# Hybrid SSD and attention layer: order of the input norm's first tiles, of the forward pass's state, and of the DMA that adds the backward part

## The chip, the cores and the metric

One core of a Trainium2 chip runs the whole layer. The time is the device time of one execution in microseconds; several executions are measured and the median is given. The engines are TensorE (PE, matrix products, with PEld for its weight loads), VectorE (DVE), ScalarE (ACT), GpSimd (POOL) and SyncE (SP, which only issues DMAs). POOL issues DMAs as well; those that add into their destination are issued by POOL alone in this kernel.

## The reference

```python
h = rms_norm(x, norm_in_g)                       # x: 1024 tokens x 1024
proj = h @ w_in                                  # z, xbc, dt, q, k, v, ga
xbc = silu(conv5(xbc) + conv_b)                  # xs (1024), B and C (2 groups x 128)
dt = softplus(dt + dt_bias); A = -exp(a_log)
y = ssd(xs, dt_f, A_f, B, C)                     # chunks of 128, forward
  + rev(ssd(rev(xs), rev(dt_b), A_b, rev(B), rev(C)))   # backward
  + d_skip * xs
y_ssd = rms_norm(y * silu(z))                    # per group of 512
o = windowed_gqa(q, k, v, rel_bias, sink)        # 16 heads, 4 kv heads, window 128
y_attn = rms_norm(o * silu(ga))
out = rms_norm(x + concat(y_ssd, y_attn) @ w_out)
```

In `ssd`, chunk c gives `y(c) = M(c) xs(c) + exp(cs) C(c) S(c)`, with M the masked scores in the chunk, and the state goes on as `S(c+1) = decay * S(c) + B(c)^T (w * xs(c))`. All of it is float32.

## The kernel before, in words

The sequence of 1024 tokens is cut into 8 blocks (chunks) of 128. Every large product is made three times from float32r halves (hi·hi, hi·lo, lo·hi), so each operand is split: ACT copies to hi, DVE or POOL subtracts to lo (`load_split`, L129 to L138, for the weights: wraw, whi, wlo).

*Start.* SP loads x in eight tiles (`xts`: xt0, then pieces of the tile xk, xt5, CT, BT) and between them two weight pieces (after the second and third tile), L196 to L202. POOL issues six small DMAs ahead of its other work: four tables broadcast to 128 rows by `rows` (sink, dsk, dtb, Ab; L183 to L185), a mask msk (L192) and later rb (L188). For each tile of x the sum of squares ss is made (DVE for the first, L212, ACT for the others, L215), then the reciprocal root rs by `rsqrt` (DVE L117, POOL L118), and DVE scales the tile in place (L218). PE transposes it into PSUM banks (L220); two tiles share the banks; ACT makes hhi (L224) and DVE hlo (L225) from them, and four early projection halves follow on PE (L146).

*The two groups.* The SSD heads form two groups g of eight heads. For each group the conv makes xk, BT, CT, Bk, and d_skip's part goes to the scratch yb_d in DRAM (L532). A backward pass over the chunks (L574 to L584) adds its part to yb_d by a DMA that accumulates (L579). Then the forward pass (L620 to L657) does, for chunk c: `scores(c+1)` makes the next M (SP loads two tables cb by broadcast, L592; ACT and DVE work on them, L607 to L617); `y_off` multiplies C with the state S (PE L570) and DVE scales the result into the tile yb (L572); a DMA of POOL adds yb_d into yb (L630); the products y with M run on PE (L635) and DVE adds them to yb (L637); `advance` makes the next state: POOL weights xd (L542), ACT and DVE split it to xh and xl (L545, L546), PE makes three products (L552), POOL scales the old state (L557) and DVE adds (L558). At last POOL multiplies yb with the gate zt to yg (L643), which is stored to y_d (L644), ACT squares it (L646), POOL folds the squares to sqs (L647, L649), and PE sums four chunks' sqs at a time (`add_sums`, L519). In the first chunk, which has no state yet, SP loads yb from yb_d (L627).

`fill(n)` puts n half blocks of the remaining projections (24 products of PE each, "fills" below, L146) between these steps, so that PE has work while the chain of a chunk goes on. The attention and the output projection come after the second group.

The order on each engine isn't that of the code: a scheduler places the instructions by its own estimate of their times, and `tc.issue_after(i)` holds back what is written under it until instruction i is placed. Tiles come from pools with a number of buffers; a tile's next use waits until its last user is done. yb has three buffers, xh and xl one each, zt and yg one each.

Of the kernel before, what the change touches and what calls it, by code (L numbers as in the profile page):

```python
# [10 lines left out]
F32 = mybir.dt.float32  # L11
F32R = mybir.dt.float32r
AF = mybir.ActivationFunctionType
ALU = mybir.AluOpType
PSUM = bass.MemoryType.PSUM

P = 128
S = 1024
D = 1024
NSB = S // P  # L20
# [4 lines left out]
NH = 16  # L25
NKV = 4
EPS = 1e-6
NEG = -1e30
# [7 lines left out]
def kernel(  # L36
# [18 lines left out]
    nc = tc.nc  # L55
    V, A, G, T = nc.vector, nc.scalar, nc.gpsimd, nc.tensor
# [15 lines left out]
    yb_d = scratch("yb_d", [NG, NSB, P, 512], F32)  # L72
# [22 lines left out]
    nhalf = const.tile([P, 16], F32, name="nhalf")  # L95
# [19 lines left out]
    def rsqrt(dst, src, scale, eps):  # L115
        n = src.shape[1]
        V.tensor_scalar(out=dst, in0=src, scalar1=scale, scalar2=eps, op0=ALU.mult, op1=ALU.add)  # L117
        G.tensor_tensor(out=dst, in0=dst, in1=nhalf[:, 0:n], op=ALU.pow)  # L118


    pa = ctx.enter_context(ExitStack())
# [7 lines left out]
    def load_split(src, shape, wpool, tag="w", eng=None):  # L129
        raw = wpool.tile(shape, F32, tag=tag + "raw", name=tag + "raw", bufs=1 if tag != "w" else 3)  # L130
        nc.sync.dma_start(out=raw, in_=src)
        hi = wpool.tile(shape, F32R, tag=tag + "hi", name=tag + "hi")
        lo = wpool.tile(shape, F32R, tag=tag + "lo", name=tag + "lo")
        A.activation(out=hi, in_=raw, func=AF.Copy)  # L134
        nsplit[0] += 1
        eng = eng or (G if nsplit[0] % 3 == 0 else V)
        eng.tensor_tensor(out=lo, in0=raw, in1=hi.bitcast(F32), op=ALU.subtract)  # L137
        return hi, lo  # L138
# [27 lines left out]
    gp = pool(ssd, "gp", side="right")  # L166
# [8 lines left out]
    s1 = pool(s1c, "s1", side="right")  # L175
# [3 lines left out]
    def rows(t, src, n):  # L179
        G.dma_start(out=t, in_=bass.AP(tensor=src.tensor, offset=src.offset, ap=[[0, P], [1, n]]))  # L180
        return t

    both = rows(s1.tile([P, NH], F32, name="sink2"), sink, NH), rows(s1.tile([P, NH], F32, name="dsk2"), d_skip, NH)  # L183
    dtb = rows(s1.tile([P, 32], F32, name="dtb"), dt_bias, 32)
    Ab = rows(s1.tile([P, 32], F32, name="Ab"), a_log, 32)  # L185
    rb = s1.tile([64, NH], F32, name="rb")
    G.memset(rb, NEG)
    G.dma_start(out=rb[0:32], in_=rel_bias)  # L188

    dsk = gp.tile([P, NH // 2], F32, name="dsk")  # L190
    msk = gp.tile([P, 2, P], F32, name="msk")
    G.dma_start(out=msk, in_=c_tri)  # L192
    xts = [cp.tile([P, S + 4], F32, tag="pad", name="xt0")[:, 0:D]]
    xts += [tiles[3][:, 2 * i:2 * i + 2, :].rearrange("p b e -> p (b e)") for i in range(4)]
    xts += [cp.tile([P, S + 4], F32, tag="pad", name="xt5")[:, 0:D], tiles[1], tiles[0]]
    for sb, xt in enumerate(xts):  # L196
# [3 lines left out]
        if sb in (1, 2):  # L200
            blk = XBC0 + 6 + 2 * sb
            pre[blk] = load_split(w_blk[blk], [P, NKB, P], wp, eng=V)  # L202
    whi, wlo = load_split(w_vdt, [P, NKB, 288], s1, tag="wv", eng=G)
    for q in range(4):
        sh, o = divmod(q, 2)
        cols = slice(o * 256, o * 256 + 256)
        banks = [bank(t) for t in ("mm t s y", "t s t s", "t s t s", "t s y t")[q].split()]
        for j, xt in enumerate(xts[2 * q:2 * q + 2]):
            junk = cp.tile([P, D], F32, tag="acc", name="junk")
            ss = s1.tile([P, 1], F32, tag="ss", name="ss", bufs=8)  # L210
            if q == j == 0:
                V.tensor_tensor_reduce(out=junk, in0=xt, in1=xt, scale=1.0, scalar=0.0, op0=ALU.mult,  # L212
                                       op1=ALU.add, accum_out=ss)
            else:
                A.activation(out=junk, in_=xt, func=AF.Square, accum_out=ss)  # L215
            rs = s1.tile([P, 1], F32, tag="rs", name="rs", bufs=8)
            rsqrt(rs, ss, 1.0 / D, EPS)
            V.tensor_scalar(out=xt, in0=xt, scalar1=rs, scalar2=None, op0=ALU.mult)  # L218
            for kb in range(NKB):
                T.transpose(banks[kb // 2][:, (kb % 2) * 256 + j * P:(kb % 2) * 256 + (j + 1) * P],  # L220
                            xt[:, kb * P:(kb + 1) * P], ident)
        for kb in range(NKB):
            ps = banks[kb // 2][:, (kb % 2) * 256:(kb % 2) * 256 + 256]
            A.activation(out=hhi[sh][:, kb, cols], in_=ps, func=AF.Copy, scale=g_in[:, kb:kb + 1])  # L224
            V.scalar_tensor_tensor(out=hlo[sh][:, kb, cols], in0=ps, scalar=g_in[:, kb:kb + 1],  # L225
                                   in1=hhi[sh][:, kb, cols].bitcast(F32),
                                   op0=ALU.mult, op1=ALU.subtract)
        for blk, ws in pre.items():
            if o == 0:
                early.setdefault(blk, []).append(bank("mm"))  # L230
            for _ in proj_steps(early[blk][sh][:, cols], ws, sh, cols):
                pass
# [42 lines left out]
    with s1c:  # L275
# [4 lines left out]
        for sb in range(NSB):  # L280
            sh, j = divmod(sb, 4)
            ps = bank("mm")
            n = 0
            for kb in range(NKB):
                for l, r in ((hhi, whi), (hlo, whi), (hhi, wlo)):
# [9 lines left out]
                              in_=vt.bitcast(F32).rearrange("p k a d -> p k (a d)"))  # L295
# [20 lines left out]
        for d in range(2):  # L316
            V.scalar_tensor_tensor(out=dt[:, d], in0=t3v[:, :, d * NH:(d + 1) * NH], scalar=2.0,
                                   in1=t2v[:, :, d * NH:(d + 1) * NH], op0=ALU.mult, op1=ALU.add)
            V.scalar_tensor_tensor(
                out=av[:, d], in0=dt[:, d], scalar=-1.0,  # L320
                in1=Ab[:, d * NH:(d + 1) * NH].unsqueeze(1).broadcast_to([P, NSB, NH]),
                op0=ALU.mult, op1=ALU.mult)
# [200 lines left out]
    for g in range(NG):  # L523
# [16 lines left out]
        def weighted(c, d):  # L540
            xd = sp.tile([P, 512], F32, tag="xd", name="xd")
            G.tensor_tensor(out=v3(xd), in0=v3(xk[:, c, :]), in1=bc(hb(wst, d, c, g), 64), op=ALU.mult)  # L542
            xh = sp.tile([P, 512], F32R, tag="xh", name="xh", bufs=1)
            xl = sp.tile([P, 512], F32R, tag="xl", name="xl", bufs=1)
            A.activation(out=xh, in_=xd, func=AF.Copy)  # L545
            V.tensor_tensor(out=xl, in0=xd, in1=xh.bitcast(F32), op=ALU.subtract)  # L546
            return xh, xl, xh

        def advance(Sold, c, d):
            ps = bank("s")  # L550
            for i, (b, x) in enumerate(zip((Bk[0], Bk[0], Bk[1]), weighted(c, d))):
                T.matmul(ps, lhsT=b[:, c, :], rhs=x, start=i == 0, stop=i == 2)  # L552
            Sn = sp.tile([P, 512], F32, tag="S", name=f"S{d}")
            if Sold is None:
                A.activation(out=Sn, in_=ps, func=AF.Copy)
            else:
                G.tensor_tensor(out=v3(Sn), in0=v3(Sold), in1=bc(hb(dec, d, c, g), 64), op=ALU.mult)  # L557
                V.tensor_tensor(out=Sn, in0=Sn, in1=ps, op=ALU.add)  # L558
            return Sn
# [25 lines left out]
        Sf = None  # L585
# [35 lines left out]
        for c in range(NSB):  # L621
            M = Mn
            if c < NSB - 1:
                Mn = scores(c + 1)
            yb = sp.tile([P, 512], F32, tag="yo", name="yb", bufs=3)
            if Sf is None:
                nc.sync.dma_start(out=yb, in_=yb_d[g, c])  # L627
            else:
                y_off(Sf, c, 0, yb)
                G.dma_start(out=yb, in_=yb_d[g, c], accum_op=ALU.add)  # L630
            fill(FORWARD[c][0])
            py = bank("y")
            for h in range(HPG):
                a = h % 2 * 64
                T.matmul(py[a:a + 64, h // 2 * P:(h // 2 + 1) * P], lhsT=xk[:, c, h * 64:(h + 1) * 64],  # L635
                         rhs=M[:, h, :], start=True, stop=True)
            V.tensor_tensor(out=yb, in0=py, in1=yb, op=ALU.add)  # L637
            if c < NSB - 1:
                Sf = advance(Sf, c, 0)
            zt = sp.tile([P, 4, P], F32, tag="zt", name="zt", bufs=1)  # L640
            nc.sync.dma_start(out=zt, in_=z_d[g * 4:(g + 1) * 4, :, c * P:(c + 1) * P].rearrange("b p s -> p b s"))
            yg = sp.tile([P, 512], F32, tag="yg", name="yg", bufs=1)
            G.tensor_tensor(out=yg, in0=yb, in1=zt.rearrange("p b s -> p (b s)"), op=ALU.mult)  # L643
            nc.sync.dma_start(out=y_d[g, c], in_=yg)  # L644
            y2 = sp.tile([P, 512], F32, tag="y2", name="y2", bufs=1)
            A.activation(out=y2, in_=yg, func=AF.Square)  # L646
            G.tensor_tensor(out=y2[:, 0:256], in0=y2[:, 0:256], in1=y2[:, 256:512], op=ALU.add)  # L647
            sqs = sp.tile([P, P], F32, tag="sqs", name="sqs", bufs=6)
            G.tensor_tensor(out=sqs, in0=y2[:, 0:P], in1=y2[:, P:256], op=ALU.add)  # L649
            sums.append((g, c, sqs))  # L650
            if c == 5:
                add_sums()
            if g == NG - 1 and c == 4:
                load_kv(0, 0)
                load_q(0, 0)
                load_q(0, 1)
            fill(FORWARD[c][1])  # L657
# [403 lines left out]
```

## Time and profile before

| | |
|---|---|
| median of 3 runs | 907.78 us (905.4 to 909.92) |
| profiled execution | 908.26 us |
| its span | 906.5 us |
| mean granted clock of PE | 0.98 |
| PE busy | 94% of the span, 4622 instructions |
| DVE, ACT, POOL busy | 69%, 52%, 33% |

The span runs from the first to the last instruction on the chip; the profiled execution's own time is some 2 us longer, for what lies around it. A granted clock of 1.00 is PE's upper level, 2.4 GHz, and 0.5 its lower, 1.2 GHz; a mean between them over a stretch says how much of it ran at the lower level. Times within the span are counted from its start.

### The profile page before, as it was taken

Reading aid. Unit: us, or ns where it says so; the run is one execution under the profiler, and the core shown is the slowest. Engines: PE = TensorE matmul, PEld = TensorE weight load, DVE = VectorE, ACT = ScalarE, POOL = GpSimd, SP = SyncE. Lnnn points to the kernel's source line nnn. Section 1 sums busy time; section 2 is a strip of 40 time slices with the busy share of each in tenths; the row PEclk is TensorE's granted clock in tenths of the full one; section 3 lists DMA queues with packets and bytes.
Section 4 is the critical chain, followed back from the end, with each engine's and each line's share of the span. In section 5 each row is a group of like instructions: output and inputs, shape, how many; then the busy total and the mean of one; then the engine's idle time right before and its main releaser. Section 6 shows DMA issues by size and latency. Waiting matters only on the chain.

```text
span 906.5 us, 13315 instructions
## 1 busy us (share of the span) xinstructions
PE 853.0 (94%) x4622; PEld 720.2 (79%) x4622; DVE 623.7 (69%) x1035; ACT 469.3 (52%) x1078; POOL 296.6 (33%) x271
## 2 busy tenths in 40 slices
PE   4999999998998999999969999999999899898997
PEld 3998788886777888888857888877888688787886
DVE  4575665696898476447869936687888877875533
ACT  5632573453666345423645536766566566753222
POOL 4301012534764201234268450130441340432501
PEclk9999999999899999999988999999999999998999
DMA  8122563576888413678859859789656637422421
GB/s 301 67 83 58 180 213 121 150 211 182 228 240 267 127 46 93 160 195 195 223 147 278 223 184 283 211 231 307 181 151 190 187 108 189 159 63 96 148 81 49
DMA packets 127407, 154.24 MB, mean 170 GB/s; under 512 B 42331, under 2 KB 79899, under 8 KB 127212
## 3 DMA queue, kind: packets, MB, share of 16 engines
q1 hardware_dynamic: 121420, 141.35, 50.9%
q0 software_dynamic: 5776, 11.79, 7.4%
q8 instruction: 36, 0.59, 0.3%
q14 instruction: 31, 0.25, 0.1%
q10 hardware_dynamic: 144, 0.26, 0.1%
HBM read 111.58 MB, written 43.88 MB: 171 GB/s over the span
## 4 chain that ended last, share of the span: by engine, by line
PE 64%; DVE 13%; DMA 12%; issue 4%; ACT 2%; POOL 2%; SPq 1%; POOLq 0%; DVEq 0%; ACTq 0%
PE mm L146 30%; PE mm L695 17%; PE y L913 4%; PE s L877 3%; DMA cb<-cs_d 3%; PE mm L286 3%; PE t L891 2%; DMA yb<-yb_d 2%; DMA oraw<-in_w_out_dram 2%; DVE hlo L434 2%; DMA zt<-z_d 2%; DMA yb_d<-yo 1%; DMA xk<-in_x_dram 1%; PE s L570 1%; DVE M L616 1%
## 5 line engine op out<-in xcount | busy, mean ns | idle before, releaser
L146 PE MATMUL mm<-hhi,whi 128*128 128x512 f32 (+1 forms) x640 | 248.1, 390 | 1.5 <-ACT hhi L224 1.5
L146 PE MATMUL mm<-hlo,whi 128*128 128x512 f32 (+1 forms) x640 | 247.4, 388 | 0.2 <-DVE hlo L225 0.2
L146 PE MATMUL mm<-hhi,wlo 128*128 128x512 f32 (+1 forms) x640 | 247.1, 387 | 0.0
L146 PEld LDWEIGHTS mm<-hlo,whi 128*128 128x128 f32 x640 | 122.3, 191 | 23.0 <-issue 1.7
L146 PEld LDWEIGHTS mm<-hhi,whi 128*128 128x128 f32 x640 | 121.9, 192 | 23.4 <-ACT hhi L224 2.2
L146 PEld LDWEIGHTS mm<-hhi,wlo 128*128 128x128 f32 x640 | 122.4, 191 | 22.1 <-issue 0.7
L695 PE MATMUL mm<-hlo,yh 128*128 128x512 f32 (+1 forms) x264 | 105.8, 401 | 0.0
L695 PE MATMUL mm<-hhi,yl 128*128 128x512 f32 (+1 forms) x264 | 105.8, 401 | 0.0
L695 PE MATMUL mm<-hhi,yh 128*128 128x512 f32 (+1 forms) x264 | 105.8, 401 | 0.0
L883 ACT ACTIVATE lg<-lg,nm 128x320 f32<-128x320 f32 (+2 forms) x128 | 68.7, 537 | 41.5 <-DVE nm L880 39.4
L250 DVE SCALAR_TENSOR_TENSOR acc<-pad,prm_sb,acc 128x1024 f32<-128x1024 f32 x48 | 62.1, 1300 | 24.7 <-ACT acc L247 23.3
L880 DVE CUSTOM_DVE_ANT_0 lg<-s,bias,nsnk 128x320 f32<-128x320 f32 (+2 forms) x128 | 64.4, 519 | 21.3 <-PE s L877 20.5
L134 ACT ACTIVATE whi<-wraw 128x1024 fp32r<-128x1024 f32 x38 | 40.0, 1054 | 40.7 <-PE mm L146 37.7
L137 POOL TENSOR_TENSOR wlo<-wraw,whi 128x1024 fp32r<-128x1024 f32 x12 | 30.2, 2516 | 89.9 <-ACT whi L134 89.9
L695 PEld LDWEIGHTS mm<-hhi,yl 128*128 128x128 f32 x264 | 50.9, 193 | 5.9
L695 PEld LDWEIGHTS mm<-hlo,yh 128*128 128x128 f32 x264 | 51.1, 193 | 5.8
L607 ACT ACTIVATE cb<-cb,ncs 128x128 f32<-128x128 f32 x128 | 39.4, 390 | 31.0 <-DMA cb<-cs_d 28.9
L695 PEld LDWEIGHTS mm<-hhi,yh 128*128 128x128 f32 x264 | 50.8, 193 | 5.6
L137 DVE TENSOR_TENSOR wlo<-wraw,whi 128x1024 fp32r<-128x1024 f32 x26 | 33.8, 1298 | 23.4 <-ACT whi L134 20.8
L897 DVE TENSOR_TENSOR pl<-t,ph 128x512 fp32r<-128x512 f32 (+1 forms) x64 | 40.8, 652 | 9.1 <-ACT ph L896 8.4
L877 PE MATMUL s<-khh,qt 128*128 128x320 f32 (+1 forms) x128 | 39.7, 316 | 6.9 <-DVE nm L880 6.9
L941 POOL DMA_DIRECT2D rd_d<-rdt x8 | 4.4, 555 | 116.2 <-ACT rdt L940 116.2
(232 smaller groups left out, 1766.9 us busy)
## 6 DMA issues: line engine op xcount, KB each, us to landing
wraw<-in_w_blk_dram SPq DMA_DIRECT2D x38, 512.0 KB, 4.0
cb<-cs_d SPq DMA_DIRECT2D x32, 512.0 KB, 5.8
qt<-q_d SPq DMA_DIRECT2D x32, 256.0 KB, 4.0
oraw<-in_w_out_dram SPq DMA_DIRECT2D x32, 256.0 KB, 3.8
et<-es_d SPq DMA_DIRECT2D x56, 128.0 KB, 4.9
yb_d<-pad SPq DMA_DIRECT2D x8, 512.0 KB, 3.8
z_d<-gz SPq DMA_DIRECT2D x16, 256.0 KB, 3.8
zt<-z_d SPq DMA_DIRECT2D x16, 256.0 KB, 3.6
```

Of the source, the lines that this page charges most:

```text
L134: A.activation(out=hi, in_=raw, func=AF.Copy)
L137: eng.tensor_tensor(out=lo, in0=raw, in1=hi.bitcast(F32), op=ALU.subtract)
L146: yield T.matmul(ps, lhsT=l[:, kb, :], rhs=r[sh][:, kb, cols], start=(n == 0), stop=(n == 3 * NKB - 1))
L250: V.scalar_tensor_tensor(out=acc, in0=pad[:, k:k + S], scalar=cw[:, blk * 6 + k:blk * 6 + k + 1], in1=acc, op0=ALU.mult, op1=ALU.add)
L286: T.matmul(ps[:, 0:288], lhsT=l[sh][:, kb, j * P:(j + 1) * P], rhs=r[:, kb, :], start=(n == 0), stop=(n == 3 * NKB - 1))
L607: A.activation(out=E[:, h, :], in_=E[:, h, :], func=AF.Identity, bias=ncs[:, 0, c, hh:hh + 1])
L695: yield T.matmul(ps[:, cols], lhsT=l[:, j * P:(j + 1) * P], rhs=r[:, dh * 512 + cols.start:dh * 512 + cols.stop], start=first and n == 0, ...
L877: pe(lambda: T.matmul(ps[:, 0:c1 - c0], lhsT=self.qt[:, sub, 2 * hp:2 * hp + 2, :], rhs=kt[:, k0:k0 + c1 - c0], start=(i == 0), stop=(i == ...
L880: V.tensor_tensor_reduce(out=l, in0=ps[:, d0 - c0:d1 - c0], in1=bias[:, hp, d0 - f0:d1 - f0], scale=-1.0, scalar=nsnk[:, sk], op0=ALU.add, ...
L883: A.activation(out=l, in_=l, func=AF.Exp, scale=-1.0, bias=nm, accum_out=sm)
L897: V.tensor_tensor(out=pl[0:w, 0:n], in0=ps[0:w, 0:n], in1=ph[0:w, 0:n].bitcast(F32), op=ALU.subtract)
L913: pe(lambda: T.matmul(self.po[:, sub * 256:(sub + 1) * 256], lhsT=v, rhs=r[0:v.shape[0], c:c + 256], start=i == 1 and n == 0 and j == 0, s ...
```

## The change

Three things are moved.

1. The small tables' DMAs are issued by a function, `small_tables`, under `issue_after` of the first tile's root; and every further tile's root and scale are held until the tile before is scaled.
2. In the forward pass `advance` is written right behind `y_off`, ahead of the fills and of the products y. xh and xl get two buffers.
3. The DMA that adds yb_d into yb comes after the products' add, right ahead of the load of zt and of yg. The first chunk has no SP load any more: DVE copies its products to yb, and the DMA adds yb_d to them like in the other chunks.

```diff
     def rsqrt(dst, src, scale, eps):
...
-        G.tensor_tensor(out=dst, in0=dst, in1=nhalf[:, 0:n], op=ALU.pow)
+        return G.tensor_tensor(out=dst, in0=dst, in1=nhalf[:, 0:n], op=ALU.pow)
...
+    def small_tables():
+        both = rows(s1.tile([P, NH], F32, name="sink2"), sink, NH), rows(s1.tile([P, NH], F32, name="dsk2"), d_skip, NH)
+        dtb = rows(s1.tile([P, 32], F32, name="dtb"), dt_bias, 32)
+        Ab = rows(s1.tile([P, 32], F32, name="Ab"), a_log, 32)
+        rb = s1.tile([64, NH], F32, name="rb")
+        G.memset(rb, NEG)
+        G.dma_start(out=rb[0:32], in_=rel_bias)
+
+        dsk = gp.tile([P, NH // 2], F32, name="dsk")
+        msk = gp.tile([P, 2, P], F32, name="msk")
+        G.dma_start(out=msk, in_=c_tri)
+        return both, dtb, Ab, rb, dsk, msk
...
             rs = s1.tile([P, 1], F32, tag="rs", name="rs", bufs=8)
-            rsqrt(rs, ss, 1.0 / D, EPS)
-            V.tensor_scalar(out=xt, in0=xt, scalar1=rs, scalar2=None, op0=ALU.mult)
+            with ExitStack() as st:
+                if scaled is not None:
+                    st.enter_context(tc.issue_after(scaled.ins))
+                root = rsqrt(rs, ss, 1.0 / D, EPS)
+                scaled = V.tensor_scalar(out=xt, in0=xt, scalar1=rs, scalar2=None, op0=ALU.mult)
+            if q == j == 0:
+                with tc.issue_after(root.ins):
+                    both, dtb, Ab, rb, dsk, msk = small_tables()
...
-            xh = sp.tile([P, 512], F32R, tag="xh", name="xh", bufs=1)
-            xl = sp.tile([P, 512], F32R, tag="xl", name="xl", bufs=1)
+            xh = sp.tile([P, 512], F32R, tag="xh", name="xh")
+            xl = sp.tile([P, 512], F32R, tag="xl", name="xl")
...
             yb = sp.tile([P, 512], F32, tag="yo", name="yb", bufs=3)
-            if Sf is None:
-                nc.sync.dma_start(out=yb, in_=yb_d[g, c])
-            else:
+            first = Sf is None
+            if not first:
                 y_off(Sf, c, 0, yb)
-                G.dma_start(out=yb, in_=yb_d[g, c], accum_op=ALU.add)
+            if c < NSB - 1:
+                Sf = advance(Sf, c, 0)
             fill(FORWARD[c][0])
...
-            V.tensor_tensor(out=yb, in0=py, in1=yb, op=ALU.add)
-            if c < NSB - 1:
-                Sf = advance(Sf, c, 0)
+            if first:
+                V.tensor_copy(yb, py)
+            else:
+                V.tensor_tensor(out=yb, in0=py, in1=yb, op=ALU.add)
+            G.dma_start(out=yb, in_=yb_d[g, c], accum_op=ALU.add)
             zt = sp.tile([P, 4, P], F32, tag="zt", name="zt", bufs=1)
```

The order on DVE at the start, before. xt0 is the first tile of x, xk the next pieces, rs their roots, wlo the two early weight pieces.

```order
L117 TENSOR_SCALAR rs_171<-ss_169 128x1
L117 TENSOR_SCALAR rs_186<-ss_184 128x1
L218 TENSOR_SCALAR xt0_134<-xt0_134,rs_171 128x1024
L137 TENSOR_TENSOR wlo_143<-wraw_140,whi_142 128x1024
L218 TENSOR_SCALAR xk_116<-xk_116,rs_186 128x1024
L117 TENSOR_SCALAR rs_271<-ss_269 128x1
L218 TENSOR_SCALAR xk_116<-xk_116,rs_271 128x1024
L137 TENSOR_TENSOR wlo_150<-wraw_147,whi_149 128x1024
L225 SCALAR_TENSOR_TENSOR hlo0_101<-mm_164,prm_sb_76,hhi0_99 128x256
```

The same place after the change (the lines of the new file are some ten higher).

```order
L117 TENSOR_SCALAR rs_157<-ss_155 128x1
L225 TENSOR_SCALAR xt0_120<-xt0_120,rs_157 128x1024
L117 TENSOR_SCALAR rs_186<-ss_184 128x1
L137 TENSOR_TENSOR wlo_129<-wraw_126,whi_128 128x1024
L137 TENSOR_TENSOR wlo_136<-wraw_133,whi_135 128x1024
L225 TENSOR_SCALAR xk_116<-xk_116,rs_186 128x1024
L117 TENSOR_SCALAR rs_271<-ss_269 128x1
L225 TENSOR_SCALAR xk_116<-xk_116,rs_271 128x1024
L117 TENSOR_SCALAR rs_286<-ss_284 128x1
L235 SCALAR_TENSOR_TENSOR hlo0_101<-mm_150,prm_sb_76,hhi0_99 128x256
```

The first tile's scale now stands ahead of the second's root, and both wlo ahead of the second tile's scale.

The order on ACT at the start, before: the squares (junk, ss), the hi halves of the weight pieces and the first pieces of hhi.

```order
L215 ACTIVATE junk_183,ss_184<-xk_116 128x1024
L134 ACTIVATE whi_142<-wraw_140 128x1024
L215 ACTIVATE junk_268,ss_269<-xk_116 128x1024
L134 ACTIVATE whi_149<-wraw_147 128x1024
L224 ACTIVATE hhi0_99<-mm_164,prm_sb_76 128x256
L224 ACTIVATE hhi0_99<-t_165,prm_sb_76 128x256
L215 ACTIVATE junk_283,ss_284<-xk_116 128x1024
L224 ACTIVATE hhi0_99<-s_166,prm_sb_76 128x256
```

And after.

```order
L219 ACTIVATE junk_183,ss_184<-xk_116 128x1024
L134 ACTIVATE whi_128<-wraw_126 128x1024
L219 ACTIVATE junk_268,ss_269<-xk_116 128x1024
L134 ACTIVATE whi_135<-wraw_133 128x1024
L219 ACTIVATE junk_283,ss_284<-xk_116 128x1024
L219 ACTIVATE junk_366,ss_367<-xk_116 128x1024
L234 ACTIVATE hhi0_99<-mm_150,prm_sb_76 128x256
L234 ACTIVATE hhi0_99<-t_151,prm_sb_76 128x256
L219 ACTIVATE junk_381,ss_382<-xt5_121 128x1024
```

Two more squares now stand ahead of the first piece of hhi; the two later ones in the old order stood between its pieces.

The order on POOL at the end of the second forward pass (g = 1, chunks 5 to 7), before. yb_4447, yb_4562 and yb_4672 are the tiles yb of chunks 5, 6 and 7, S0 the state.

```order
L630 DMA yb_4562<-yb_d_66 128x512
L643 TENSOR_TENSOR yg_4483<-yb_4447,zt_4481 128x512
L647 TENSOR_TENSOR y2_4486<-y2_4486 128x256
L649 TENSOR_TENSOR sqs_4489<-y2_4486 128x128
L643 TENSOR_TENSOR yg_4634<-yb_4562,zt_4632 128x512
L647 TENSOR_TENSOR y2_4637<-y2_4637 128x256
L649 TENSOR_TENSOR sqs_4640<-y2_4637 128x128
L137 TENSOR_TENSOR wlo_4783<-wraw_4780,whi_4782 128x1024
L630 DMA yb_4672<-yb_d_66 128x512
L643 TENSOR_TENSOR yg_4731<-yb_4672,zt_4729 128x512
L647 TENSOR_TENSOR y2_4734<-y2_4734 128x256
L649 TENSOR_TENSOR sqs_4737<-y2_4734 128x128
```

And after, from chunk 5's yg on.

```order
L655 TENSOR_TENSOR yg_4483<-yb_4447,zt_4481 128x512
L659 TENSOR_TENSOR y2_4486<-y2_4486 128x256
L661 TENSOR_TENSOR sqs_4489<-y2_4486 128x128
L651 DMA yb_4562<-yb_d_66 128x512
L655 TENSOR_TENSOR yg_4634<-yb_4562,zt_4632 128x512
L659 TENSOR_TENSOR y2_4637<-y2_4637 128x256
L661 TENSOR_TENSOR sqs_4640<-y2_4637 128x128
L137 TENSOR_TENSOR wlo_4783<-wraw_4780,whi_4782 128x1024
L651 DMA yb_4672<-yb_d_66 128x512
L655 TENSOR_TENSOR yg_4731<-yb_4672,zt_4729 128x512
L659 TENSOR_TENSOR y2_4734<-y2_4734 128x256
L661 TENSOR_TENSOR sqs_4737<-y2_4734 128x128
```

Each accumulating DMA stood a chunk ahead of the yg that reads its tile; now yg stands right behind it. On PE, the last product of `add_sums` (L519 on the last chunk's sqs) stood 33 fills behind the last y products of this pass; now 51 fills and four short products of the attention (L877) lie between them.

## Rows read from the trace of the kernel before

**Rows 1.** The page, part 1: busy time of each engine.

```profile
PE 853.0 (94%) x4622; PEld 720.2 (79%) x4622; DVE 623.7 (69%) x1035; ACT 469.3 (52%) x1078; POOL 296.6 (33%) x271
```

**Rows 2.** Timeline of DVE at the start: start, duration, operation, idle before.

```profile
12.95 0.74 DVE L218 TENSOR_SCALAR xk<-xk,rs 128x1024 f32<-128x1024 f32 x1
...
17.02 1.22 DVE L137 TENSOR_TENSOR wlo<-wraw,whi 128x1024 fp32r<-128x1024 f32 x1
```

**Rows 3.** Timeline of ACT at the start.

```profile
14.27 1.06 ACT L215 ACTIVATE junk<-xk 128x1024 f32<-128x1024 f32 x1 [2.57 <-DMA xk<-in_x_dram]
...
16.31 0.46 ACT L224 ACTIVATE hhi<-mm,prm_sb 128x256 fp32r<-128x256 f32 x1
```

**Rows 4.** Timeline of POOL at the start.

```profile
5.64 0.56 POOL L118 TENSOR_TENSOR rs<-rs,nhalf 128x1 f32<-128x1 f32 x1 [1.01 <-DVE rs L117]
```

**Rows 5.** Windows at the start: busy time by engine, granted clock, DMA share, GB/s.

```profile
4.00:9.00 5.00, 0.00 (x0) 0.00 (x0) 1.42 (x4) 0.00 (x0) 1.88 (x7) 1.00 0.81 232
...
14.00:22.00 8.00, 6.24 (x25) 5.14 (x25) 5.80 (x14) 7.73 (x16) 1.73 (x5) 1.00 1.03 415
```

**Rows 6.** Windows of the two forward passes, and of projections between them.

```profile
212.00:290.00 78.00, 69.12 (x394) 55.30 (x393) 65.50 (x71) 43.53 (x107) 49.51 (x40) 0.96 0.80 233
...
432.00:537.00 105.00, 97.21 (x525) 78.82 (x523) 77.75 (x92) 57.08 (x138) 58.80 (x49) 0.95 0.77 210
...
300.00:325.00 25.00, 25.00 (x116) 20.78 (x115) 14.01 (x13) 9.53 (x12) 2.54 (x3) 1.00 0.32 90
```

**Rows 7.** Waits of PE, 187 to 300 us: line, releaser, total, times, longest.

```profile
PE y L635 <- DVE yb L637: 2.4, 1, 2.4
PE s L570 <- DVE S L558: 2.3, 2, 1.9
PE y L635 <- DVE M L617: 2.0, 1, 2.0
```

**Rows 8.** Waits of PE, 432 to 540 us.

```profile
PE y L635 <- DVE yb L637: 3.0, 2, 1.8
...
PE s L570 <- DVE S L558: 1.9, 1, 1.9
```

**Rows 9.** Line L630, the accumulating DMA: time from issue to landing.

```profile
DMA to landing us min/median/max: 4.1/5.8/7.2
```

**Rows 10.** Waits of DVE, 187 to 300 us.

```profile
DVE cb L608 <- DMA cb<-cs_d: 6.0, 4, 2.6
DVE wlo L137 <- POOL y L647: 2.5, 1, 2.5
```

**Rows 11.** Groups of POOL, 432 to 537 us: count, busy us, mean ns, idle before.

```profile
L643 POOL TENSOR_TENSOR yg<-yb,zt 128x512 f32<-128x512 f32 x8 | 13.9, 1734 | 15.6 <-DVE yb L637 13.5 <-DMA zt<-z_d 2.0
L557 POOL TENSOR_TENSOR S<-S,dec 128x512 f32<-128x512 f32 x7 | 11.4, 1628 | 3.3 <-ACT S L555 2.6 <-DVE S L558 0.6
L647 POOL TENSOR_TENSOR y<-y 128x256 f32<-128x256 f32 x8 | 8.3, 1043 | 4.5 <-ACT y L646 4.5
L649 POOL TENSOR_TENSOR sqs<-y 128x128 f32<-128x128 f32 x8 | 7.7, 962 | 0.4
L542 POOL TENSOR_TENSOR xd<-xk,wst 128x512 f32<-128x512 f32 x6 | 6.6, 1092 | 5.0 <-DVE xl L546 5.0
...
L137 POOL TENSOR_TENSOR wlo<-wraw,whi 128x1024 fp32r<-128x1024 f32 x2 | 5.2, 2586 | 0.0
```

**Rows 12.** Timeline of POOL at the end of the second forward pass.

```profile
533.72 1.27 POOL L643 TENSOR_TENSOR yg<-yb,zt 128x512 f32<-128x512 f32 x1 [5.23 <-DVE yb L637]
535.72 0.74 POOL L647 TENSOR_TENSOR y<-y 128x256 f32<-128x256 f32 x1 [0.74 <-ACT y L646]
536.54 0.46 POOL L649 TENSOR_TENSOR sqs<-y 128x128 f32<-128x128 f32 x1
```

**Rows 13.** Timeline of PE: first y products and last sum, second forward pass.

```profile
459.37 1.09 PE L635 MATMUL y<-M,xk 128*64 128x128 f32 x16 [1.81 <-DVE yb L637]
...
537.06 0.38 PE L519 MATMUL t<-ones,sqs 128*128 128x1 f32 x2
```

More of the change, by code (lines that the diff above doesn't have):

```diff
@@ L181, in rows @@
         return t
[L183 to L192, printed above, removed]
+    def small_tables():
[9 more added lines that the diff above has]
+        return both, dtb, Ab, rb, dsk, msk
     xts = [cp.tile([P, S + 4], F32, tag="pad", name="xt0")[:, 0:D]]
@@ L203 @@
     whi, wlo = load_split(w_vdt, [P, NKB, 288], s1, tag="wv", eng=G)
+    scaled = None
     for q in range(4):
```

## The prediction

> **What bounds the kernel now.** The page's first part comes first: TensorE (PE) is busy 853.0 us of the span's 906.5, DVE 623.7, POOL 296.6 [rows 1]. So what a change can win from PE is its 53 us of idle time and the time at its lower clock, and one asks where those lie in the stretches that the change touches: the start and the two forward passes.
>
> The start is read from the timelines. DVE ends x1's scale at 13.7 and spends 1.22 us on the second weight piece's lo after it [rows 2]. ACT has waited 2.57 us for x2 when it squares it at 14.27, and makes its first piece of hhi at 16.31 [rows 3]. POOL takes the first root at 5.64, behind the issues of the small tables [rows 4]. While these move, transfers run at 232 GB/s (4 to 9 us), against 415 GB/s in 14 to 22 us [rows 5].
>
> The forward passes are read from the windows and then from the waits. In 212 to 290 (first group, "g0" below) PE is busy 69.12 of 78 us at a granted clock of 0.96, DVE 65.50, POOL 49.51; in 432 to 537 (second group, "g1") PE 97.21 of 105 at 0.95 [rows 6]. PE waits there for yb, for the state S and once for M: in g0 2.4, 2.3 and 2.0 us, in g1 3.0 for yb and 1.9 for S [rows 7, 8]. Behind the first two stands one thing: DVE's add at L637 waits for the accumulating DMA, which lands 4.1 to 7.2 us after its issue, 5.8 in the middle [rows 9], and the state's add L558 and the next M are queued behind it on DVE. In 300 to 325, where PE never waits, its granted clock is 1.00 [rows 6].
>
> **The change part by part.** The profiled execution took 908.26 us, 0.5 over the median of the three runs; the sum is made against 908.3. About 0.5% (903.2 to 912.3) is what a measurement of this kernel can tell from no change.
>
> *Start.* Every row of x and every weight is still loaded, scaled and split; only the order moves. x0's scale leaves the wait for x1's root, which alone gains nothing: the first hhi reads a bank that holds x0 and x1. What counts is x1. It gains if the tables, issued behind the first root from 6.2 us on (5.64 + 0.56) [rows 4], no longer slow its load; the root loses nothing, since only the tables stand behind it on POOL. x1 loses in two places of the new order: the second lo of 1.22 us, and so the second weight piece's arrival, is now ahead of its scale on DVE, and two more squares of 1.06 us are ahead of the first hhi on ACT [rows 2, 3]. Best case: 5 us at 232 instead of 415 GB/s are 2.2 us of transfers, and as much again behind them: some −4. Worst case: all arrives as before, so the second hi ends at 16.4 (14.27 + two operations of 1.06), its lo at 17.6, x1's scale of 0.74 at 18.4 instead of 13.7, and the first hhi begins some 0.5 later, 18.9 instead of 16.3: +2.6. I take −1, near the middle, since the squares made early aren't made later between pieces of hhi.
>
> The rows show that loads are slow while the tables move, not where the tables would cost less. The Trainium skill ("DMA: Bandwidth & Descriptors", section "Issuing engines are not separate DMA queues") says that DMAs of all issuing engines run on the same 16 DMA engines and interleave. By that the tables cost their time wherever they stand, the second weight piece would be hit in x1's place, and the start would be the worst case; rows 5 agree in that the sum of both kinds of transfer falls to 232 GB/s.
>
> *State early.* On PE the three products of advance now come right behind y_off; on DVE the state's add no longer stands behind the add of yb. The waits addressed in g0 are 2.4 + 2.3 + 2.0 = 6.7 us, and the lower clock costs (1 − 0.96) × 78 = 3.1: together 9.8. In g1: 3.0 + 1.9 + (1 − 0.95) × 105 = 10.1. Not all of it can come. PE at full clock needs 69.12 − 3.1 = 66.0 us of the 78 in g0, DVE 65.50, so two nearly equal engines take turns; and DVE waits 6.0 us for the cb tables and 2.5 for a weight split [rows 10], so that it alone would need 74.0, 4.0 less than the 78. Between nothing and 9.8 I take half, near that: −4.9 in g0, and −5.0 in g1.
>
> *Second buffers for xh and xl.* ACT may write the next xh before PE has read the last. PE's waits for xl are not counted in the sum, neither gone nor grown.
>
> *Copies and loads.* Two adds of DVE become two copies of the same size, two loads of SP become DMAs of POOL: 0, beside PE's fills; without that cover 0.7 us each.
>
> *The accumulating DMA last.* This is the new wait. Before, its landing ran beside the fills, and POOL sat idle 13.5 us for yb in g1 [rows 11]. Now it is issued behind the products' add, and in four of the eight chunks yg follows it at once on POOL's queue, so POOL waits out the landing with S, y2, sqs and weight splits queued behind. PE needs the last chunk's sqs at the end of g1, for the sum L519. So the POOL chain is added up from the first y there. By the mean rows: eight landings 8 × 5.8 = 46.4; eight yg 8 × 1.73 = 13.9; and what lies outside a landing in the new order, four S at 1.63, two xd at 1.09, six y2 at 1.04, five sqs at 0.96, one split at 2.59 and four waits of 0.74 for ACT's square, 25.4; with 1.8 from the start of the first y's products to the first issue (PE 1.09 and some 0.7 for DVE's copy) 87.5 [rows 9, 11, 12, 13]. Lower end: each landing the shortest, 4.1, and yg 1.27, y2 0.74, sqs 0.46 as in the last chunk [rows 9, 12]: 32.8 + 10.2 + 21.0 + 1.8 = 65.8. I take two thirds of the way, since the same engines are busy beside it: 80.1.
>
> PE before went 537.06 − 459.37 = 77.7 us from the first y to the last sum [rows 13]. The new order puts 51 fills ahead of that sum behind the last y where 33 stood, 18 more at 25.00 / 116 = 0.216 us [rows 6], and four short products: 4.5 more, 82.2; less the 5.0 gained, 77.2. So PE waits 2.9 us at the sum, and g1 nets −2.1. Ends: no wait, or 10.3. In g0 the same lag falls under projections that don't need sqs: 0; if that cover fails, the next weight split of POOL is late.
>
> The Trainium skill (the same page, section "Anatomy of one DMA — SWDGE (gpsimd) path") gives 2.0 us and bytes / 436e3, an estimate of 2.6 us for these 256 KB. By that the chain is 25 us shorter, the sum never waits, and the total is 898. The trace differs: 5.8 in the middle and never under 4.1 [rows 9], which decides.
>
> Sum: 908.3 − 1 − 4.9 − 2.1 = 900.3, so **900**.
>
> **The rivals.**
> *All of it comes:* no wait returns, and POOL runs at its lower end: 908.3 − 1 − 9.8 − 10.1 = 887. For it: all these waits hang on one add. Against: DVE's share of g0.
> *DVE takes over:* M is late in yb's place, DVE's waits for cb and the split come through to PE: g0 −9.8 + 8.5 = −1.3, g1 with half of its −2.1: 905. For it: PE waits 2.0 us for M already [rows 7]. Against: fills stand between, and PE need not follow DVE's every wait.
> *POOL sets the pace (slower):* the chain takes its mean rows, 87.5. PE waits 10.3 us at the last sum and runs behind that at the lower clock, 1.6 (half of g0's 3.1): g1 is −5.0 + 10.3 + 1.6 = +6.9. In g0 the next weight split stands behind yg on POOL and comes late, which eats the 4.9: 908.3 − 1 + 6.9 = 914. It decides once the chain exceeds 82.2 (77.2 and the 5.0); with the other means that is a landing of 5.1 us. For it: yg right behind its DMA. Against: POOL's operations are short where DVE is idle, as in rows 12.
> *The tables cost as much in their new place:* the start is +2.6, and the sum 908.3 + 2.6 − 7.0 = 904.
> *The change does less than it says:* the order hid the add already: 908.
>
> **How the numbers follow.** Forecast 0.40, all of it 0.12, DVE 0.16, POOL 0.18, tables 0.11, nothing 0.03. The forecast's own range, with start and chain half way to their ends, is 896 to 905. Faster by over 0.5% (below 903.2): most of the forecast, all of the second, some of the tables' case: 0.52. Slower (above 912.3): most of POOL's case: 0.15. Within 0.5%: 0.33. The range, 887 to 913, leaves out the lower half of the second case and half of POOL's.
>
> **What would show it.** Right: PE no longer waits for yb at the y products; POOL idles before yg on DMA yb rather than on DVE; PE waits 1 to 6 us at the last sum; the first hhi begins at 15 to 16 us. Wrong: the first hhi past 18 (tables); PE waiting for M, or DVE for cb, by more than 9 us (DVE); 10 us of wait at the sum or PE behind POOL's splits (POOL); no wait at the sum at all (the chain is mis-sized).

## The result: 0.8% slower, outside the range

The changed kernel takes 915.63 us in the median of 5 runs (913.48 to 917.62) beside 907.77 for the kernel before: a ratio of 1.0076, 95% interval 1.0047 to 1.0105. The forecast was 900, with a range of 887 to 913. The profiled execution has a span of 913.9 us, 7.4 more than before.

**Busy time and windows.** The engines are busy for nearly as long as before: this is the page's first part after, and the windows that answer to [rows 1] and [rows 6].

```profile
PE 853.4 (93%) x4622; PEld 719.2 (79%) x4622; DVE 625.4 (68%) x1035; ACT 467.5 (51%) x1078; POOL 298.7 (33%) x273
```

```profile
212.00:290.00 78.00, 69.34 (x402) 55.91 (x401) 66.34 (x72) 41.78 (x107) 47.04 (x36) 0.96 0.75 214
432.00:537.00 105.00, 96.08 (x532) 77.15 (x531) 81.31 (x95) 54.60 (x135) 55.79 (x46) 0.95 0.78 210
```

In the first window PE is busy a little longer than before (69.34 us against 69.12), in the second less long (96.08 against 97.21), at the same clock. So other waits stand where the old ones went. Better than by windows, which lie at fixed times, the two are compared at places that both programs pass in the same order: the later kernel is 2.5 us behind when the first backward pass begins, 6.4 behind when the second group's transposes begin, 6.1 when the attention begins, and 7 to 8 within it. In this execution, then, the first group's passes lose 3.9 us, and the second group's neither lose nor gain.

**PE's waits after**, both passes (187 to 300 and 432 to 550 us, as all waits by pass below), columns as in [rows 7, 8]:

```profile
PE s L580 <- DVE S L568: 6.6, 2, 4.8
PE mm L146 <- DVE qlo L387: 3.0, 1, 3.0
PE y L645 <- DVE yb L648: 1.2, 1, 1.2
PE y L645 <- DVE yb L650: 0.8, 1, 0.8
...
PE s L580 <- DVE S L568: 8.1, 3, 5.1
```

PE hardly waits for yb any more (2.0 us in the first pass, in two pieces; nothing in the second), as forecast. It waits for S instead: 6.6 and 8.1 us, where before it was 2.3 and 1.9. L568 is the state's add, L558 before.

**The waits of POOL and SP after.** POOL's yg now waits for the DMA:

```profile
POOL yg L655 <- DMA yb<-yb_d: 27.1, 7, 7.0
...
POOL yg L655 <- DMA yb<-yb_d: 30.6, 8, 6.6
```

and SP's queue waits for POOL's yg, since the store of yg to y_d and the load of zt are issued by SP. Before:

```profile
SPq L644 <- POOL yg L643: 13.3, 6, 3.6
...
SPq L644 <- POOL yg L643: 20.4, 7, 5.8
```

and after:

```profile
SPq L656 <- POOL yg L655: 35.0, 7, 9.6
...
SPq L656 <- POOL yg L655: 35.4, 8, 6.9
```

From 33.7 us in both passes together to 70.4. Behind that store, on the same queue, stand the loads of cb, of et (the factors of y_off) and of weights. DVE's wait for cb in the first pass, 6.0 us in [rows 10], is now

```profile
DVE cb L618 <- DMA cb<-cs_d: 12.9, 5, 3.0
DVE cb L619 <- ACT cb L617: 5.5, 3, 2.6
```

One such place in the trace of after, all engines in order of time. SP issues nothing from 219.9 to 226.0; then yg is there, and the store, zt and cb go out in a burst. DVE waits 3.04 us for cb, and the state's add, behind M, a split and yb in DVE's queue, begins at 241.03, for which PE has waited 4.78 us:

```profile
218.81 1.09 SPq L576 DMA_DIRECT2D et<-es_d  x2
...
223.97 2.00 POOL L655 TENSOR_TENSOR yg<-yb,zt 128x512 f32<-128x512 f32 x1 [2.50 <-DMA yb<-yb_d]
...
226.00 0.33 SPq L656 DMA_DIRECT2D y_d<-yg  x1
...
226.38 0.43 SPq L653 DMA_DIRECT2D zt<-z_d  x1
...
226.89 0.52 SPq L602 DMA_DIRECT2D cb<-cs_d  x1
...
227.98 0.66 SPq L602 DMA_DIRECT2D cb<-cs_d  x1
...
232.86 1.42 DVE L618 TENSOR_TENSOR cb<-cb,ncs 128x1024 f32<-128x1024 f32 x1 [3.04 <-DMA cb<-cs_d]
...
236.30 1.95 DVE L627 TENSOR_TENSOR M<-M,cb 128x1024 f32<-128x1024 f32 x1
...
241.03 0.67 DVE L568 TENSOR_TENSOR S<-S,s 128x512 f32<-128x512 f32 x1
...
241.75 1.65 PE L580 MATMUL s<-CT,S 128*128 128x128 f32 x6 [4.78 <-DVE S L568]
```

How much of the 3.04 us is due to SP's idle time this one place doesn't tell (the cb tiles must also have been read by M); the run with SP's queue freed does.

**The start.** Tables behind the root did free x1: its square begins at 7.22 us, not 9.35. But now the fifth tile of x pays (the fourth piece of xk). ACT waits for it, with the first piece of hhi behind:

```profile
16.54 1.06 ACT L219 ACTIVATE junk<-xk 128x1024 f32<-128x1024 f32 x1 [1.92 <-DMA xk<-in_x_dram]
...
17.59 0.46 ACT L234 ACTIVATE hhi<-mm,prm_sb 128x256 fp32r<-128x256 f32 x1
```

The first hhi begins at 17.59, where [rows 3] have 16.31.

### The profile page after: what moved, and what is told of

Same layout as the page of the kernel before. It is cut to its first block, busy times and chain, and to the rows that moved or that the text cites. A ratio compares the mean times of both kernels' runs of the same rounds, so it can differ in the third digit from the quotient of the medians.

```text
span 913.9 us, 13317 instructions
## 1 busy us (share of the span) xinstructions
PE 853.4 (93%) x4622; PEld 719.2 (79%) x4622; DVE 625.4 (68%) x1035; ACT 467.5 (51%) x1078; POOL 298.7 (33%) x273
## 4 chain that ended last, share of the span: by engine, by line
PE 60%; DVE 14%; DMA 13%; issue 6%; ACT 4%; POOL 2%; SPq 1%; DVEq 0%; POOLq 0%; ACTq 0%
PE mm L146 27%; PE mm L707 17%; DMA cb<-cs_d 3%; PE y L925 3%; PE s L889 3%; PE mm L296 3%; PE t L903 2%; DMA oraw<-in_w_out_dram 2%; DVE hlo L444 2%; DVE M L627 1%; DVE M L626 1%; DMA xk<-in_x_dram 1%; PE s L580 1%; ACT cb L617 1%; DMA yb_d<-pad 1%
## 5 line engine op out<-in xcount | busy, mean ns | idle before, releaser
L580 PE MATMUL s<-CT,S 128*128 128x128 f32 x224 | 32.7, 292 | 14.9 <-DVE S L568 14.7
L580 PEld LDWEIGHTS s<-CT,S 128*128 128x128 f32 x224 | 30.4, 203 | 19.3 <-DVE S L568 17.0
```

What stands on the lines that cost most here:

```text
L580: T.matmul(ps[:, b * P:(b + 1) * P], lhsT=Sx[:, b * P:(b + 1) * P], rhs=CT[:, c * P:(c + 1) * P], start=True, stop=True)
```

## The experiments

All were timed in turn with the kernel before, on one chip for each group; the ratios are to it.

**One part at a time.** Three kernels: the new start alone; the early state with both second buffers, the DMA ahead of the products as before; both changes of the forward passes with the old start. The second one's edit:

```diff
-            xh = sp.tile([P, 512], F32R, tag="xh", name="xh", bufs=1)
-            xl = sp.tile([P, 512], F32R, tag="xl", name="xl", bufs=1)
+            xh = sp.tile([P, 512], F32R, tag="xh", name="xh")
+            xl = sp.tile([P, 512], F32R, tag="xl", name="xl")
...
                 G.dma_start(out=yb, in_=yb_d[g, c], accum_op=ALU.add)
+            if c < NSB - 1:
+                Sf = advance(Sf, c, 0)
             fill(FORWARD[c][0])
...
             V.tensor_tensor(out=yb, in0=py, in1=yb, op=ALU.add)
-            if c < NSB - 1:
-                Sf = advance(Sf, c, 0)
```

> The new start alone (tables behind the first root, scales in order), forward passes as before. Theory: in the trace of after the same work comes 2.0 to 2.5 us later from the second projection on, so this kernel takes about 910.2, with the first piece of hhi at 17 to 18 us and all the loss ahead of 80 us. Rival: the late start is taken up by slack before the backward pass and the whole loss is the forward passes': 907.8.

> State early and two buffers for xh and xl, but the DMA that adds yb_d stays ahead of the products, and the start as before. If the late DMA does the harm (by SP's or by POOL's queue), this one isn't slower: 904 to 908, PE waits little for S, SP waits for yg as before (13 us in the first pass, not 35). Rival, that the early state itself does harm (its add and xl stand in DVE's queue in front of M): 911 or more, with PE waiting for M or S over 8 us.

> Both changes of the forward passes, with the start as before. Theory: the losses add, so 915.6 less the start's 2.5: about 913, and the wait of SP for yg is again near 35 us in each pass. Rival, that the losses come from one another (a late start moves the passes into other transfers): 908 to 910.

Measured: the start alone 1.0003 (0.9978 to 1.0027), the early state with buffers 0.9863 (0.9823 to 0.9902), both forward changes 1.0042 (1.0018 to 1.0066). The start alone is not measurably slower; its profile had the first hhi at 16.42 and no delay by 80 us, while after showed 2.0. So the delay differs between executions, and the theory (910.2 beside 907.8, a ratio of 1.0026) is neither shown nor, at the edge of the interval, ruled out. The second, the early state with both buffers, gains more than forecast, 897.1 against 909.59, and its windows show it: PE is busy 2.8 us longer in the first, at a clock of 1.00. By the places that all pass in the same order it gains 7.1 us from the first backward pass to the second group's transposes, and 4.7 more up to the attention.

```profile
212.00:290.00 78.00, 71.94 (x423) 58.60 (x424) 67.83 (x72) 47.45 (x118) 47.26 (x39) 1.00 0.83 240
432.00:537.00 105.00, 99.44 (x549) 82.33 (x548) 82.92 (x103) 56.25 (x139) 61.08 (x50) 0.95 0.79 220
```

With the DMA last, that gain is gone and more: 912.12 − 897.1 = 15.0 us between the second and the third kernel, measured side by side. By the same places the third kernel loses 3.7 us in the first group's passes and 3.1 in the second's, so that more of the difference lies in the first (10.8 us against 7.8 in the profiled executions, which part by more there than the medians do). As the start costs nothing that shows, the late DMA is the whole harm.

**SP's queue freed.** The kernel after, with the two transfers that wait for yg moved to POOL's queue, behind yg itself:

```diff
-            nc.sync.dma_start(out=zt, in_=z_d[...])
+            G.dma_start(out=zt, in_=z_d[...])
...
-            nc.sync.dma_start(out=y_d[g, c], in_=yg)
+            G.dma_start(out=y_d[g, c], in_=yg)
```

> The kernel after, with the store of yg and the load of zt issued on POOL's queue, so that nothing on SP waits for yg; POOL gets two issues of 0.9 us more per chunk. Theory A (SP's queue: the loads of cb, et and weights stand behind the store that waits for yg): the forward passes win back 4 or more, 909 to 912, DVE's and ACT's waits for cb fall below those of before. Theory B (POOL's own queue: S, xd and weight splits stand behind yg): 14 us of issues more in each pass's chain, 918 to 930, and PE waits for S longer than 15 us.

Measured: 0.9977 (0.9952 to 1.0003), 908.4 us. In the first pass SP no longer waits for POOL's yg; its longest waits there are for DVE:

```profile
SPq L602 <- DVE M L626: 14.6, 6, 5.9
SPq L576 <- DVE yb L582: 12.4, 5, 4.6
```

DVE's wait for cb in the first pass falls from 12.9 to 5.2 us, though POOL has 32 more issues, and PE's waits for S in both fall from 6.6 + 8.1 = 14.7 to 4.6 us. Theory A holds, B as stated falls: beside the ratio of 1.0076 for after, about 1% came back. Of what is left, a part shows on PE as a new wait for POOL; over the whole span:

```profile
PE t L529 <- POOL sqs L661: 7.0, 3, 4.7
...
PE s L580 <- DVE S L568: 4.6, 2, 2.5
```

The 7.0 us are sums waiting for POOL's sqs, with POOL's queue longer still. They are a wait of the kind that the prediction put at the end of the second pass, but at other places: 4.7 us stand at 262 us and 2.1 at 501, at the sums of each pass's first four chunks, and the last sum, at 544, waits for nothing.

**The tail a chunk later.** Both forward changes with the old start, and yg's part of chunk c held back until the DMA of chunk c + 1 is issued, so that nothing stands waiting behind a DMA just issued:

```diff
+            added = G.dma_start(out=yb, in_=yb_d[g, c], accum_op=ALU.add)
+            if c > 0:
+                with tc.issue_after(added.ins):
+                    finish(c - 1, ybp)
+            ybp = yb
```

(`finish` holds the lines from zt's load to `sums.append`; the last chunk's follows the loop.)

> Both changes of the forward passes with the old start, and the tail of a chunk (load of zt, yg, its store, squares) held back until the next chunk's DMA is issued, so that yg comes a chunk behind the DMA it needs. Theory: the late DMA does harm only through what stands behind the waiting yg, on SP's and POOL's queues: 897 to 902, the waits of SP for yg below 20 us per pass. Rival, that the DMA itself is in the way at its new time (its traffic against cb's loads): 908 or more with those waits gone.

Measured: 0.9916 (0.9886 to 0.9946), 900.8 us, with the two waits of SP at

```profile
SPq L625 <- POOL yg L624: 13.8, 6, 5.8
...
SPq L625 <- POOL yg L624: 15.2, 7, 5.1
```

against 36.0 and 41.3 in the kernel with the same two changes and the tail in its old place (1.0042). So most of the harm is not in the DMA's new time but in what waits for it in order. Whether the new time does a little harm of its own isn't shown: 0.9916 lies above the 0.9863 of the early state with both buffers and the DMA ahead, but the intervals overlap.

**Which part of the second kernel gains.** Five more kernels: the start and the early state together; the early state with one buffer each; the early state with xh's second buffer alone; the buffers alone, on the kernel before; xl's second buffer alone, on the kernel before.

> The new start and the early state, the DMA as before ahead of the products. If parts add, the start's 0 (1.0003) and the state's 0.986: about 897, 894 to 900. Rival: the start's 2 us, which two of the three profiles with it show by 80 us, are real when nothing later swallows them: 899 to 901, and the next pass begins 2 us later than in the run with the early state alone.

> The early state without the second buffers of xh and xl, DMA and start as before. Theory: the order of advance carries the gain and the buffers little: 897 to 900. Rival: the early state needs them, since xh of the next chunk is made while PE still reads the last: 903 to 908, with waits of ACT or DVE for the products L552.

> The kernel before with nothing changed but the second buffers of xh and xl; advance is written behind the products and the DMA stands ahead of them. Theory: the early state of the run that gained (0.986) came from the buffers, since with one buffer each the scheduler already set the products of advance right behind y_off in most chunks: 896 to 901, in the same places (6 us by the end of the first pass, 4 in the second). Rival, that buffers and the early place are both needed: 905 to 910.

> The early state with a second buffer for xh alone, xl with one. PE reads xh in the first and the last of the three products, xl in the second. If ACT's write of xh ahead of PE's last product is what the buffers free: 896 to 901. If DVE's xl is what binds, since it then still waits for PE before the next chunk's xl: 905 to 910.

> The kernel before with a second buffer for xl alone. The run with xh's alone stayed at 1.00. If xl's buffer carries the gain (DVE can make it before PE has read the last chunk's), 896 to 901. Rival, that only both together let the three products stand in one piece behind y_off: 905 to 910.

| kernel | ratio | interval |
|---|---|---|
| start, early state, both buffers | 0.9875 | 0.9840 to 0.9911 |
| early state, one buffer each | 1.0017 | 0.9994 to 1.0041 |
| both buffers alone | 0.9883 | 0.9842 to 0.9924 |
| early state, xh's buffer alone | 1.0011 | 0.9986 to 1.0036 |
| xl's buffer alone | 0.9994 | 0.9967 to 1.0022 |

The expectation for one buffer each missed (both its cases lay below the 910.24 us measured); those for the buffers alone and for the start with the early state held. The buffers carry the gain, and only both together. The place of advance in the code does little; in the trace of before, PE's products of advance stand right behind y_off in most chunks already. What the buffers move is the split: on DVE, before, the fifth forward xl stands where with both buffers the next chunk's stands, one chunk further ahead. Before:

```order
L546 TENSOR_TENSOR xl_2319<-xd_2316,xh_2318 128x512
L368 SCALAR_TENSOR_TENSOR gz_2229<-gth_2227,mm_2202 128x512
L617 TENSOR_TENSOR M_2099<-M_2099,cb0_2090 128x1024
L637 TENSOR_TENSOR yb_2122<-y_2163,yb_2122 128x512
```

With both buffers:

```order
L546 TENSOR_TENSOR xl_2432<-xd_2429,xh_2431 128x512
L368 SCALAR_TENSOR_TENSOR gz_2229<-gth_2227,mm_2202 128x512
L617 TENSOR_TENSOR M_2099<-M_2099,cb0_2090 128x1024
L637 TENSOR_TENSOR yb_2122<-y_2163,yb_2122 128x512
```

(xl_2432 belongs to the chunk after that of xl_2319.) The traces bear this out: counted on DVE from the start of a group's backward pass, ten splits stand ahead of the first product add in each of the four kernels with both buffers and the DMA ahead of the products (ratios of 0.9846 to 0.9883), and nine in the kernel before and in those with one second buffer or none (but eight, where the DMA comes last as well). That the split can't run ahead while one of the two tiles is single, since xl is made from xh, fits this.

How the order becomes 1.2% isn't shown. PE's waits for xl, before

```profile
PE s L552 <- DVE xl L546: 1.5, 2, 1.4
...
PE s L552 <- DVE xl L546: 2.5, 3, 0.9
```

don't occur in the kernel with both buffers, but neither do they occur with the early state and xh's buffer alone, which gains nothing (1.0011). So these waits by themselves are not the gain. Nor is the order all of it: the kernel with the tail a chunk later has nine splits there and still gains 0.8%.

**The last DMA alone, and SP freed in another way.** First the DMA last with the state made behind the products and one buffer each; then the kernel after with the store of yg on POOL, two buffers for zt and one for xh.

> The DMA last alone: the state is made behind the products as before, one buffer of xh and xl, old start. Theory: the waiting yg blocks SP and POOL whatever the place of advance, so the loss shows without the early state's gain to set against it: 914 to 922. Rival, that the late DMA is harmful only together with the early state: 904 to 909, since here too DVE's add no longer waits for the DMA.

> The kernel after with the store of yg on POOL's queue and two buffers for zt, paid for by xh's second buffer, so that SP waits for no yg of the same chunk and POOL gets only one issue of 0.9 us more per chunk. If SP's queue is the larger part of the late DMA's cost: 900 to 907, SP's waits for yg below 5 us per pass. If POOL's own queue is: 910 or more, with POOL idle before yg as in after (27 to 31 us per pass) and PE waiting for S or the sums as there. A third case is that xh's buffer matters here: waits of PE for the products L562.

Measured: 1.0046 (1.0022 to 1.0069), as the theory had it in kind, but less in size (912.19 where 914 to 922 stood). So the cost of the late DMA is no fixed sum: about 0.5% with one buffer each, and 1.8% with two, since with the DMA last the early state and the buffers gain nothing (1.0042 against 1.0046). Why they gain nothing there wasn't tested further. The kernel after with the store on POOL's queue took 1.0049 (1.0021 to 1.0076), which tells nothing of SP's part, because SP wasn't freed: the load of zt now waited in the store's place, in the first and in the second pass

```profile
SPq L653 <- POOL yg L655: 42.4, 7, 9.8
...
SPq L653 <- POOL yg L655: 20.5, 4, 8.6
```

and with one buffer for xh PE waited 11.5 us for xl. How the late DMA's 15 us divide between SP's queue and POOL's therefore stays open; the run with both transfers on POOL's queue shows only that SP's part is large: it won back about half of the 2% between 0.9875 (start, early state, buffers; above) and 1.0076, with POOL's queue made longer.

**A version that beats both.** Start, early state and both buffers, the DMA ahead of the products, and the fourth tile's square behind the fourth piece of hhi (the fifth's, which lands late, follows it on ACT and is held back with it; the expectation names the fourth for both):

```diff
+                    if q == j == 1:
+                        st.enter_context(tc.issue_after(hh0.ins))
                     A.activation(out=junk, in_=xt, func=AF.Square, accum_out=ss)
```

> Early state, both second buffers, the DMA ahead of the products, the new start, and the fourth tile's square held back until four pieces of hhi are made, so that ACT doesn't wait for that tile (it lands at 16.5 us with the new start) before the first piece. Theory: the new start's loss is this wait on ACT; the first piece of hhi begins at 14.5 to 16 us, all that follows about 1.5 us earlier than in the run with start and state: 894 to 897. Rival, that PE then waits for the later tiles instead: 897 as that run, with waits of PE for scaled tiles between 18 and 24 us.

Measured: 0.9846 (0.9807 to 0.9886), 893.6 us, the lowest median of all. ACT's first hhi there:

```profile
15.29 0.48 ACT L237 ACTIVATE hhi<-mm,prm_sb 128x256 fp32r<-128x256 f32 x1 [2.70 <-PE mm L233]
```

That is 2.3 us earlier than in after. Against the same kernel without the edit (0.9875) the intervals overlap, so its gain is seen in the trace and not in the time.

## Why the prediction was wrong

*The term that failed is "The accumulating DMA last".* It was charged 2.9 us, for one wait at the last sum, and nothing in the first pass ("0"). It cost 15.0 us (912.12 against 897.1), more than half of it in the first group's passes, and most of it by taking away the buffers' gain. The step looked for who stands behind the waiting yg on POOL's queue and stopped there. Next to yg stand two transfers of SP that need it, and SP's queue too goes in order (it issued nothing from 219.9 to 226.0 above): "loads of SP" appear in the text only as two that go away. The wait then reached PE as a wait for S, through cb and DVE: with SP's queue freed, DVE's wait for cb and PE's for S fell together.

*The chain's total was met by its mean rows, and missed by the mix with the low end.* In after, POOL goes from the first of these DMAs to the last sqs

```profile
463.07 0.89 POOL L651 DMA_DIRECT2D yb<-yb_d  x1 [2.05 <-issue]
...
547.37 0.46 POOL L661 TENSOR_TENSOR sqs<-y 128x128 f32<-128x128 f32 x1
```

in 547.37 + 0.46 − 463.07 = 84.8 us, where the mean rows gave 85.7 (87.5 less the 1.8 ahead of the first issue) and the text took 80.1 with the 1.8. The landing is as before, 5.7 us in the middle. That the totals agree is in part luck: POOL idled 30.6 us for the landings, where the text had 46.4 of them in the chain, and other work and waits filled the rest. Yet PE doesn't wait at that sum in after: it had been made late by S and comes at 548.13, 0.3 us after POOL is done. One reading was wrong besides: the products at 459.37 in [rows 13] are the second chunk's; the first chunk's stand at 426.98, during the backward pass. And two sums are slightly off: two thirds of the way from 65.8 to 87.5 is 80.3, not 80.1, and without a wait at the sum the total is 897.4, not 898. Neither changes the forecast by more than 0.2 us.

*"State early" gained, for another reason.* −9.9 was forecast in both passes before the tail's charge; the kernel with that part alone gained 12.5 (909.59 − 897.1). But the place of advance, to which the text gave it, is worth nothing that shows (1.0017 with one buffer), and the buffers, which the text left out of the sum, 1.2%. So a gain of the forecast's size came from a part that the text had put at nothing, and its nearness to 9.9 is luck. The waits for xl, 1.5 and 2.5 us, were in the trace as a sign that the split was held up, but pricing them would have given 4.0 us and not 12.5.

*The start's* −1 against 0 within 0.25%: inside its bounds. The two squares ahead of hhi did what the text feared, by the fifth tile's arrival rather than the second weight piece's. The slow stretch moved along with the tables: 334 GB/s in 4 to 9 us and 258 in 9 to 14, where it was 232 and 310, and another tile is the one that waits. The Trainium skill ("DMA: Bandwidth & Descriptors", section "Issuing engines are not separate DMA queues") says that DMAs of all issuing engines run on the same 16 DMA engines and interleave; the trace agrees. The line of before for 9 to 14 us, and the two of after:

```profile
9.00:14.00 5.00, 2.22 (x9) 1.82 (x10) 2.77 (x4) 2.21 (x3) 3.02 (x5) 1.00 0.96 310
...
4.00:9.00 5.00, 1.97 (x8) 1.57 (x8) 2.32 (x6) 1.64 (x3) 3.43 (x7) 1.00 0.95 334
9.00:14.00 5.00, 0.00 (x0) 0.00 (x0) 3.06 (x4) 3.30 (x5) 1.36 (x5) 1.00 1.10 258
```

*The rivals.* "POOL sets the pace" named 914 and came nearest in time and in direction; its place, the last sum, was wrong. In after PE waits at no sum, and where SP was freed it waits at the sums of the first four chunks. Its other condition, a loss in the first group, was right, though by SP's queue and not by a weight split of POOL. "DVE takes over" had one link of the real chain, the waits for cb, without the cause. The chances gave slower 0.15, too little: the text itself found that the chain of mean rows exceeds its deciding point, and then took two thirds.

## What to carry to other kernels

Where a wait moves onto an instruction, follow its result to every queue that takes it: a DMA that needs it holds up all later loads of the queue that issues it. If a result must wait for a DMA just issued, put work of the next step between; one chunk's distance brought back 1.25% here. And where a scheduler sets the order, a move in the source can be worth little, while a buffer that limits the order may be worth the whole gain: try the buffer alone, and each part beside the others, since here the gain of one went when the other was added.

## What was not expected

Two small tiles of 2 KB per row (xh and xl) in second copies gave 1.2% of this kernel, and either alone nothing (xh's with the early state, xl's without). And moving the small tables by 5 us changed little in how much the loads of x are slowed, only which tile is: x1's square began 2.1 us earlier, the fifth's arrival held up the first hhi by 1.9.
